# SwiGLU's hidden columns in five chunks of 512 and one mixed chunk of 256 gate and 256 up columns, in place of four of 512 and two of 384

## The chip, the cores and the metric

The kernel runs on one core of one Trainium2 chip. The metric is the device time of one execution in microseconds (us). An execution is also recorded by the hardware profiler; its page and its trace give the start and the duration of every instruction on the core's engines: TensorE (PE for matmuls, PEld for weight loads), VectorE (DVE), ScalarE (ACT), GpSimd (POOL), and SyncE (SP), which here issues loads.

## What is computed

A two-layer encoder trunk over 256 tokens of 1024 features, in float32. Each layer adds half a SwiGLU, a mixer, and half a SwiGLU to `x`; a final norm follows. Cut to what matters here:

```python
def swiglu(h, w_gate, w_up, w_down):      # 1024 x 2816, 1024 x 2816, 2816 x 1024
    return (jax.nn.silu(h @ w_gate) * (h @ w_up)) @ w_down

for layer in range(2):
    x = x + 0.5 * swiglu(rms_norm(x, ffn1_norm[layer]), ...)
    x = x + mixer(rms_norm(x, mix_norm[layer]))      # attention, even and odd layer differ
    x = x + 0.5 * swiglu(rms_norm(x, ffn2_norm[layer]), ...)
out = rms_norm(x, final_norm)
```

So there are six stages, numbered 0 to 5; the four SwiGLU stages are 0, 2, 3 and 5.

## The kernel before

**Precision by three products.** A float32 matrix product is made of three passes. Each weight is split into a high part (`hi`, a rounded copy that ACT makes, `high_part`, L461) and a low part (`lo`, the difference, by DVE, `low_part`, L464). Activations are split the same way (`th`, `tl` for the normalised input, `g_h`, `g_l` for the hidden values). `mm` (L444) then issues three matmuls into one accumulator, L453 to L455; this is a *triple*. The stationary operand is a 128 x 128 block of activations, the moving operand up to 512 columns of weights.

**The columns of a SwiGLU stage.** `ffn` (L629) goes through `FF_CHUNKS` (L31), the widths into which the 2816 hidden columns are cut. For a plain chunk it takes the 8 row blocks of the gate weights (`self.take(KD)`), runs `project` (L572) for both token tiles (128 tokens each), 8 triples each, and does the same for the up weights. `silu` (L640) runs on ACT one triple after a gate product is complete, `glu` (L644) on DVE one triple after the up product; 14 triples later (`GLU_WAIT`) the result is transposed on TensorE (`transposed`, L651) and split into `gT`, the operands of the down product. Some of the 512-wide chunks (`SEVEN`, L80: chunk 2 in stages 0 and 5, chunks 1 and 3 in stages 2 and 3) go through `seven_gates` (L729), which uses a Strassen scheme with seven products for gate and up together, and prepares sums of the input for it in `x_sums` (L699). These sums are kept in places that are needed only later: the split hidden values of later chunks (`g0_...`), and where there are fewer than four of them, a place of later pair sums (`k...`).

**The down product.** After the chunks the stage takes pairs of row blocks of `w_down` in the order of `DOWN` (L34), some as plain products, some by the Strassen scheme (`seven`, L873). The four accumulators `Y` stand in the banks `o`, `pj`, `s` and `s`.

**Banks.** `BANKS` (L121): two of `pj`, three of `s`, one `o`, two `tp`, each of 512 float32 columns; banks of one name are used in turn. A plain chunk takes `s`, `s` for the gates and `pj`, `pj` for the ups (after a Strassen chunk `pj`, `s`, `s`, `pj`).

**Supply of weights.** `plan` (L288) lists the loads in order of use. A unit is one raw tile of up to a megabyte; there are three (`RAWS`). A unit's load is issued on SP's queue by `load` (L356) when the first split of an earlier unit is begun. `supply` (L402) splits two row blocks at a time into `hi` and, a triple later, `lo`; up to seven such splits may be alive (`FIT`). How often that happens is paced by the triples: each adds `self.rate` to `self.due` in `tick` (L267), and when two blocks are due and there is room, a split is made. A split that is needed sooner is made at once. All engines run their instructions in the order in which the program issues them.

Of the kernel before, what the change touches and what calls it, by code (L numbers as in the profile page):

```python
# [17 lines left out]
P = 128  # L18
T = 256
NT = 2  # L20
D = 1024
KD = D // P
# [5 lines left out]
THETA = 10000.0  # L28
NEG = -1e30
SCALE = HD ** -0.5  # L30
FF_CHUNKS = [512, 512, 512, 512, 384, 384]  # L31


DOWN = {  # L34
# [154 lines left out]
def pairs(stage):  # L189
    return [({"p": "plain", "s": "strassen"}[o[0]], int(o[1:])) for o in DOWN[stage].split()]  # L190
# [9 lines left out]
class Trunk:  # L200
# [87 lines left out]
    def plan(self):  # L288


        a = self.a

        def columns(w2d, spans, units=None, kind="narrow"):
            w = sum(n for _, n in spans)
            k = 0
            for nk in units or (4, 4):
                pieces, o = [], 0
                for c0, n in spans:
                    src = w2d[k * P : (k + nk) * P, c0 : c0 + n].rearrange("(k p) n -> p k n", p=P)
                    pieces.append(((slice(0, P), slice(0, nk), slice(o, o + n)), src))  # L300
                    o += n
                yield pieces, nk, w, [2], kind
                k += nk

        def ffn(n, l, stage):
            c0 = 0
            for ci, w in enumerate(FF_CHUNKS):
                first = stage == 0 and c0 == 0
                if ci in SEVEN[stage]:
                    for k in range(0, KD, 2):  # L310
                        pieces = []
                        for i, name in enumerate(("_w_gate", "_w_up")):
                            src = a[n + name][l][k * P : (k + 2) * P, c0 : c0 + w].rearrange("(k p) n -> p k n", p=P)
                            pieces.append(((slice(0, P), slice(0, 2), slice(i * w, i * w + w)), src))
                        yield pieces, 2, D, [2], "strassen" if k >= KD - 2 * SEVEN[stage][ci] else "wide"
                    c0 += w
                    continue
                yield from columns(a[n + "_w_gate"][l], [(c0, w)], FIRST if first else None, "narrow" if first else "wide")
                yield from columns(a[n + "_w_up"][l], [(c0, w)], None, "wide")
                c0 += w  # L320
            for i, (kind, pair) in enumerate(pairs(stage)):
                src = a[n + "_w_down"][l][2 * pair * P : 2 * (pair + 1) * P, :].rearrange("(k p) n -> p k n", p=P)
                uses = [2, 3 if stage == 5 and i >= len(pairs(stage)) - HELD else 2]
                yield [(slice(0, P), src)], 2, D, uses, "wide" if kind == "plain" else kind

        def even():
            w_in, w_out = a["even_w_in"][0], a["even_w_out"][0]
            for spans in ([(512, 256), (1280, 256)], [(768, 512)], [(0, 512)]):
                yield from columns(w_in, spans)
            for g in (1, 0):  # L330
                for nh in range(2):
                    pieces = []
                    for s in range(2):
                        r0 = g * 512 + s * 256
                        src = w_out[r0 : r0 + 256, nh * 512 : nh * 512 + 512].rearrange("(j p) n -> p j n", p=HD)
                        pieces.append((slice(64 * s, 64 * s + 64), src))
                    yield pieces, 4, 512, [2], "narrow"

        def odd():
            w_qkv, w_out = a["odd_w_qkv"][0], a["odd_w_out"][0]  # L340
            for g in range(2):
                for i in (1, 0, 2):
                    yield from columns(w_qkv, [(i * D + g * 512, 512)])
            for g in range(2):
                for nh in range(2):
                    src = w_out[g * 512 : g * 512 + 512, nh * 512 : nh * 512 + 512].rearrange("(j p) n -> p j n", p=P)
                    yield [(slice(0, P), src)], 4, 512, [2], "narrow"

        yield from ffn("ffn1", 0, 0)
        yield from even()  # L350
        yield from ffn("ffn2", 0, 2)
        yield from ffn("ffn1", 1, 3)
        yield from odd()
        yield from ffn("ffn2", 1, 5)
# [233 lines left out]

    def first_gates(self, W):

# [29 lines left out]
        for j in range(KD // 2):  # L620
# [3 lines left out]
            for k in (2 * j, 2 * j + 1):  # L624
                for tt in range(NT):
                    self.mm(ps[tt], now.hT[tt][k], W[k], k == 0, k == KD - 1)
        return ps

    def ffn(self):  # L629
# [5 lines left out]
        tasks = []  # L635

        paired = {2 * pair: [] for kind, pair in down if kind == "strassen"}
        sums = {}

        def silu(tt, w, g, s):  # L640
            yield 1
            nc.scalar.activation(s[:, :w], g[:, :w], AF.Silu, scale=self.rstd_of(tt))

        def glu(tt, f0, w, u, s):  # L644
            yield 1
            m = self.t([P, 512], "glu", 2)
            nc.vector.scalar_tensor_tensor(m[:, :w], u[:, :w], self.now.r[tt], s[:, :w], op0=ALU.mult, op1=ALU.mult)
            yield GLU_WAIT
            yield from transposed(tt, f0, w, m)
# [49 lines left out]
        def x_sums():  # L699

            yield SEVEN_WAIT[self.now.n]
            gap = SEVEN_GAP[self.now.n]
            X = []
            for tt in range(NT):
                while len(self.now.hT[tt]) < KD:
                    yield 1
                x = self.t([P, 2, 512], ("shi", "slo")[tt], FIT["sum"], F32R).bitcast(F32)
                X.append(x.rearrange("p a (k t) -> p (a k) t", t=P)[:, : 2 * most, :])
                hi, lo = (t.bitcast(F32)[:, KD - 2 * most :, :] for t in self.hts[self.now.n, tt])
                nc.vector.tensor_tensor(X[tt], hi, lo, op=ALU.add)  # L710
                yield gap
            k0, k1, k2, k3 = (X[tt][:, i::2, :] for tt in range(NT) for i in range(2))
            for o, x, y, op in [
                (k2, k3, k2, ALU.subtract), (k3, k3, k1, ALU.subtract), (k1, k2, k1, ALU.subtract), (k0, k1, k0, ALU.add)
            ]:
                nc.vector.tensor_tensor(o, x, y, op=op)
                yield gap

            places = [(f"g0_{sum(FF_CHUNKS[:ci]) // P}_", FF_CHUNKS[ci] // P) for ci in range(max(sevens), len(FF_CHUNKS))]
            if len(places) < 4:  # L720
                places.append((f"k{max(paired)}", 4))
            for (tag, n), k in zip(places, (k0, k1, k2, k3)):
                hi, lo = (self.t([P, n, P], tag + p, 1, F32R)[:, :most, :] for p in "hl")
                self.high_part(hi, k)
                yield gap
                self.low_part(lo, k, hi)
                K.append([(hi[:, q, :], lo[:, q, :]) for q in range(most)])
# [98 lines left out]

        f0 = 0
        self.spawn(x_sums())
        for ci, w in enumerate(FF_CHUNKS):
            if ci in sevens:  # L830
                seven_gates(f0, w, sevens[ci])
                f0 += w // P
                continue
            self.rate = (AHEAD_RATE if ci + 1 in sevens else RATE)[self.now.n]

            tags = ["pj", "s", "s", "pj"] if ci - 1 in sevens else ["s", "s", "pj", "pj"]
            G = self.take(KD)
            S = []
            if self.now.n + ci == 0:
                both = self.first_gates(G)  # L840
            for tt in range(NT):
                g = both[tt] if self.now.n + ci == 0 else self.project(self.ready(tt), G, tags[tt])
                S.append(self.t([P, 512], "silu", 2))
                self.start(silu(tt, w, g, S[tt]))
            U = self.take(KD)
            for tt in range(NT):
                u = self.project(self.now.hT[tt], U, tags[NT + tt])
                tasks.append(self.start(glu(tt, f0, w, u, S[tt])))
            f0 += w // P
        W = {}  # L850

        parts = [[slice(0, 512), slice(512, 1024)] for _ in range(NT)]
# [7 lines left out]
        def use(f, tt, sl, last=False, to=None):  # L860
# [4 lines left out]
            if to is not None:  # L865
                self.mm(to, gT[tt][f], W[f][i], f == held[0], last, at)
                return
            self.mm(Y[tt][i][:, at], gT[tt][f], W[f][i], (tt, i) not in begun, last, at)
            begun.add((tt, i))
# [56 lines left out]
        for i, (kind, pair) in enumerate(down[:-HELD]):  # L926
# [6 lines left out]
            for f in (2 * pair, 2 * pair + 1):  # L933
                W[f] = self.take(2)
                for tt in range(NT):
# [6 lines left out]
        for f in held:  # L942
            W[f] = self.take(2)
        for tt in range(NT):
# [588 lines left out]
```

## Time and profile before

| | us |
|---|---|
| device time, median of 3 runs (956.24 to 956.81) | 956.25 |
| span of the profiled execution, first to last instruction | 954.4 |
| TensorE busy | 942.5 |
| VectorE busy | 791.9 |
| ScalarE busy | 585.3 |

The span of the profiled execution is 1.85 us shorter than the median of the runs, since it counts from the first to the last instruction. The page calls an engine busy while one of its instructions is under way. Matmuls overlap in it: each lasts longer than the distance to the next one's start, so that what a matmul costs in a row of matmuls is read from start to start. In a view of groups a row names the line, the engine, the operation, what it writes and reads and its shape, the count, the busy time in us and the mean of one in ns, and then the idle time of the engine ahead of it with what ended it. In a timeline a row is start, duration (of a merged row: of all its instructions), engine and line. The view by windows gives for each stretch its length, then for each engine the busy time and the number of instructions, then the granted clock, the busy share of the DMA engines and what they moved.

### The profile page before, as it was taken

Reading aid. Unit: us, or ns where it says so; the run is one execution under the profiler, and the core shown is the slowest. Engines: PE = TensorE matmul, PEld = TensorE weight load, DVE = VectorE, ACT = ScalarE, POOL = GpSimd, SP = SyncE. Lnnn points to the kernel's source line nnn. Section 1 sums busy time; section 2 is a strip of 40 time slices with the busy share of each in tenths; the row PEclk is TensorE's granted clock in tenths of the full one; section 3 lists DMA queues with packets and bytes.
Section 4 is the critical chain, followed back from the end, with each engine's and each line's share of the span. In section 5 each row is a group of like instructions: output and inputs, shape, how many; then the busy total and the mean of one; then the engine's idle time right before and its main releaser. Section 6 shows DMA issues by size and latency. Waiting matters only on the chain.

```text
span 954.4 us, 13005 instructions
## 1 busy us (share of the span) xinstructions
PE 942.5 (99%) x4767; PEld 795.7 (83%) x4767; DVE 791.9 (83%) x1244; ACT 585.3 (61%) x1011; POOL 95.3 (10%) x152
## 2 busy tenths in 40 slices
PE   9999999999999999999999999999999999999997
PEld 6888998877778889988888899888878888889886
DVE  6989777788869998787988888889877697996797
ACT  7555555477777565655646456557877585556453
POOL 1130000073420000000100000006130000000001
PEclk9999999999999999999999999999999999999999
DMA  8846665644425654766456476564624365466461
GB/s 289 267 135 204 204 214 176 218 132 94 128 89 176 216 193 143 243 220 217 145 168 199 151 217 222 198 242 137 202 97 145 121 201 196 134 207 201 165 242 44
DMA packets 82752, 171.65 MB, mean 180 GB/s; under 512 B 4096, under 2 KB 25344, under 8 KB 82688
## 3 DMA queue, kind: packets, MB, share of 16 engines
q1 hardware_dynamic: 82112, 170.04, 53.7%
q8 instruction: 37, 0.61, 0.3%
q10 hardware_dynamic: 576, 0.79, 0.2%
q14 instruction: 27, 0.22, 0.1%
HBM read 169.76 MB, written 1.05 MB: 179 GB/s over the span
## 4 chain that ended last, share of the span: by engine, by line
PE 90%; DVE 4%; ACT 3%; issue 1%; DMA 1%; POOL 1%; SPq 0%; POOLq 0%; DVEq 0%; ACTq 0%
PE pj L453 13%; PE pj L455 12%; PE pj L454 12%; PE s L454 11%; PE s L455 11%; PE s L453 11%; PE tp L531 3%; PE o L454 2%; PE o L455 2%; PE o L453 2%; PE o L1006 2%; DVE lo L464 2%; PE tp L1085 1%; PE tp L453 1%; PE tp L454 1%; PE tp L455 1%
## 5 line engine op out<-in xcount | busy, mean ns | idle before, releaser
L464 DVE TENSOR_TENSOR lo<-raw,hi 128x1024 fp32r<-128x1024 f32 (+2 forms) x388 | 375.9, 991 | 66.0 <-ACT hi L461 64.0
L461 ACT ACTIVATE hi<-raw 128x1024 fp32r<-128x1024 f32 (+2 forms) x388 | 320.5, 862 | 81.2 <-PE s L455 22.2
L453 PE MATMUL pj<-hi,th 128*128 128x512 f32 (+1 forms) x431 | 164.6, 382 | 0.0
L454 PE MATMUL pj<-lo,th 128*128 128x512 f32 (+1 forms) x431 | 161.1, 374 | 0.1
L455 PE MATMUL pj<-hi,tl 128*128 128x512 f32 (+1 forms) x431 | 161.1, 374 | 0.0
L453 PE MATMUL s<-hi,th 128*128 128x512 f32 (+1 forms) x373 | 142.0, 381 | 0.2 <-ACT hi L461 0.2
L454 PE MATMUL s<-lo,th 128*128 128x512 f32 (+1 forms) x373 | 139.0, 373 | 0.3 <-DVE lo L464 0.2
L455 PE MATMUL s<-hi,tl 128*128 128x512 f32 (+1 forms) x373 | 138.8, 372 | 0.0
L455 PEld LDWEIGHTS pj<-hi,tl 128*128 128x128 f32 x431 | 80.9, 188 | 12.2
L453 PEld LDWEIGHTS pj<-hi,th 128*128 128x128 f32 x431 | 81.0, 188 | 11.4 <-issue 0.9
L454 PEld LDWEIGHTS pj<-lo,th 128*128 128x128 f32 x431 | 81.1, 188 | 10.9 <-DVE lo L464 0.5
L454 PEld LDWEIGHTS s<-lo,th 128*128 128x128 f32 x373 | 70.2, 188 | 11.3 <-DVE lo L464 2.3
L455 PEld LDWEIGHTS s<-hi,tl 128*128 128x128 f32 x373 | 70.0, 188 | 9.8
L453 PEld LDWEIGHTS s<-hi,th 128*128 128x128 f32 x373 | 70.1, 188 | 9.3 <-ACT hi L461 0.4
L473 POOL TENSOR_TENSOR rstd<-var,mhalf 128x1 f32<-128x1 f32 (+2 forms) x16 | 17.1, 1069 | 592.7 <-DVE var L471 457.6
L461 ACT ACTIVATE shi<-two 128x1024 fp32r<-128x1024 f32 x30 | 31.8, 1059 | 41.6 <-DVE two L382 41.5
L464 DVE TENSOR_TENSOR slo<-raw,shi 128x1024 fp32r<-128x1024 f32 x30 | 36.6, 1221 | 20.5 <-ACT shi L461 20.5
L461 ACT ACTIVATE g_h<-tp 128x384 fp32r<-128x384 f32 (+1 forms) x48 | 25.7, 538 | 45.2 <-DVE quarters L679 24.4
L461 ACT ACTIVATE shi<-raw 128x1024 fp32r<-128x1024 f32 x30 | 31.7, 1058 | 33.2 <-PE s L455 19.1
L453 PE MATMUL s<-hi,g_h 128*128 128x512 f32 (+1 forms) x131 | 52.0, 397 | 0.0
L455 PE MATMUL s<-hi,g_l 128*128 128x512 f32 (+1 forms) x131 | 51.0, 389 | 0.0
L454 PE MATMUL s<-lo,g_h 128*128 128x512 f32 (+1 forms) x131 | 50.9, 388 | 0.0
(473 smaller groups left out, 1669.2 us busy)
## 6 DMA issues: line engine op xcount, KB each, us to landing
raw<-in_ffn_w_down SPq DMA_DIRECT2D x44, 1024.0 KB, 5.1
raw<-in_ffn_w_up SPq DMA_DIRECT2D x20, 1024.0 KB, 5.2
raw<-in_ffn_w_gate SPq DMA_DIRECT2D x18, 1024.0 KB, 5.1
raw<-in_ffn_w_gate SPq DMA_DIRECT2D x27, 512.0 KB, 3.9
raw<-in_ffn_w_up SPq DMA_DIRECT2D x24, 512.0 KB, 4.9
raw<-in_ffn_w_gate SPq DMA_DIRECT2D x16, 768.0 KB, 4.6
raw<-in_ffn_w_up SPq DMA_DIRECT2D x16, 768.0 KB, 4.8
raw<-in_odd_w_qkv SPq DMA_DIRECT2D x12, 1024.0 KB, 5.3
```

What stands on the lines that cost most here:

```text
L453: mm(ps, h, wh, start=first, stop=False)
L454: mm(ps, h, wl, start=False, stop=False)
L455: mm(ps, l, wh, start=False, stop=last)
L461: self.nc.scalar.activation(hi, src, AF.Copy)
L464: self.nc.vector.tensor_tensor(lo, src, hi.bitcast(F32), op=ALU.subtract)
L473: nc.gpsimd.tensor_tensor(r[:, :n], v[:, :n], self.mhalf[:, :n], op=ALU.pow)
L531: self.nc.tensor.transpose(tb[:, i * P : (i + 1) * P], src[:, i * P : (i + 1) * P], self.ident)
L1006: self.nc.tensor.matmul(O[64 * s : 64 * s + 64, i * P : i * P + P], v(b0 + i, s, kc), pT[s][:, i, kc, :], start=(kc == 0), stop=(kc == 1),)
L1085: nc.tensor.transpose(tb[:, o : o + P], p[:, i, kc * P : kc * P + P], self.ident)
```

## The change

The last two chunks of 384 columns become one of 512 and a rest of 256 (`FF_MIXED`). The rest is loaded so that one tile of 512 columns holds 256 of the gate and 256 of the up weights: two units of four row blocks, two loads each, taken after the last full chunk. One product of 8 triples per token tile fills one bank `s` with both; `silu` reads its first half and `glu` its second half. The places of `x_sums` follow the new list of chunks, and where it is too short any number of places of later pair sums is appended, the last first.

```diff
-FF_CHUNKS = [512, 512, 512, 512, 384, 384]
+FF_CHUNKS = [512, 512, 512, 512, 512]
+FF_MIXED = 256
...
                 yield from columns(a[n + "_w_gate"][l], [(c0, w)], FIRST if first else None, "narrow" if first else "wide")
                 yield from columns(a[n + "_w_up"][l], [(c0, w)], None, "wide")
                 c0 += w
+            for k in range(0, KD, 4):
+                pieces = []
+                for i, name in enumerate(("_w_gate", "_w_up")):
+                    src = a[n + name][l][k * P : (k + 4) * P, c0 : c0 + FF_MIXED].rearrange("(k p) n -> p k n", p=P)
+                    pieces.append(((slice(0, P), slice(0, 4), slice(i * FF_MIXED, (i + 1) * FF_MIXED)), src))
+                yield pieces, 4, 2 * FF_MIXED, [2], "wide"
...
             places = [(f"g0_{sum(FF_CHUNKS[:ci]) // P}_", FF_CHUNKS[ci] // P) for ci in range(max(sevens), len(FF_CHUNKS))]
-            if len(places) < 4:
-                places.append((f"k{max(paired)}", 4))
+            places += [(f"k{f}", 4) for f in sorted(paired, reverse=True)]
...
                 tasks.append(self.start(glu(tt, f0, w, u, S[tt])))
             f0 += w // P
+
+        w, V = FF_MIXED, self.take(KD)
+        for tt in range(NT):
+            both = self.project(self.now.hT[tt], V, "s")
+            s = self.t([P, 512], "silu", 2)
+            self.start(silu(tt, w, both, s))
+            tasks.append(self.start(glu(tt, f0, w, both[:, w:], s)))
         W = {}
```

## The prediction

> **What bounds the kernel now.** First the page: its head, the share of each engine, the granted clock, and the engines of the chain that ended last.
>
> ```profile
> span 954.4 us, 13005 instructions
> ...
> PE 942.5 (99%) x4767; PEld 795.7 (83%) x4767; DVE 791.9 (83%) x1244; ACT 585.3 (61%) x1011; POOL 95.3 (10%) x152
> ...
> PEclk9999999999999999999999999999999999999999
> ...
> PE 90%; DVE 4%; ACT 3%; issue 1%; DMA 1%; POOL 1%; SPq 0%; POOLq 0%; DVEq 0%; ACTq 0%
> ```
>
> TensorE is busy in 99% of the span at full clock and makes up 90% of the chain. So the change can help only if it makes TensorE's own work shorter or takes away one of its few waits; work that it saves on DVE or ACT counts only where TensorE waits for them. But matmuls overlap, so "busy" also hides short waits. I therefore look at the stretches that the change rewrites, the two chunks of 384 columns in each of the four SwiGLU stages (0, 2, 3, 5), in the view by windows:
>
> ```profile
> core 0: us, PE busy (x) PEld busy (x) DVE busy (x) ACT busy (x) POOL busy (x), PEclk, DMA share, GB/s
> 97.50:132.30 34.80, 34.80 (x207) 34.64 (x206) 23.32 (x31) 20.18 (x29) 0.00 (x0) 1.00 0.62 212
> 370.00:404.80 34.80, 34.80 (x207) 34.65 (x206) 27.78 (x41) 21.14 (x34) 0.00 (x0) 1.00 0.71 237
> 552.75:588.05 35.30, 35.26 (x207) 34.51 (x206) 29.26 (x42) 21.78 (x34) 0.00 (x0) 1.00 0.77 257
> 855.15:889.95 34.80, 34.80 (x207) 34.62 (x207) 24.83 (x35) 20.68 (x31) 0.00 (x0) 1.00 0.62 212
> ```
>
> The first number is the length of the stretch. Three stages take 34.80 us for it and stage 3 takes 35.30, so there TensorE loses 0.5 us to waits; elsewhere it runs through. DVE is busy 67 to 83% of the time: nothing here is limited by it. What one matmul really costs is the distance between starts, which the timeline of TensorE shows (stage 0, the change from 512 to 384 columns):
>
> ```profile
> 94.80 0.39 PE L453 MATMUL pj<-hi,th 128*128 128x512 f32 x1
> ...
> 97.52 0.33 PE L453 MATMUL s<-hi,th 128*128 128x384 f32 x1
> ...
> 98.59 0.33 PE L453 MATMUL s<-hi,th 128*128 128x384 f32 x1
> ...
> 101.19 0.60 PE L531 MATMUL tp<-mats,glu 128*128 128x128 f32 x4
> ```
>
> From 94.80 to 97.52 stand 12 matmuls of 512 columns, from 98.59 to 101.19 stand 15 of 384. So one of 512 takes 2.72 / 12 = 226.7 ns and one of 384 takes 2.60 / 15 = 173.3 ns. The 128 columns between them cost 53.3 ns, 0.417 ns each. By that 512 columns are 213.3 ns and 384 are 160 ns: **about 13.3 ns of each matmul do not depend on its columns.** This is the term that the change acts on.
>
> **The change part by part.** *Matmuls.* Before, the two chunks take per stage 2 chunks x 2 (gate, up) x 2 token tiles x 8 row blocks x 3 products = 192 matmuls of 384. After, a chunk of 512 takes 96 and the mixed one, with gate and up side by side in one bank, 8 x 2 x 3 = 48, all of 512: 144. The columns are the same (192 x 384 = 144 x 512 = 73,728). Times: 192 x 173.3 = 33.28 us, 144 x 226.7 = 32.64 us. Saved: 0.64 us per stage, **2.56 us in four stages**, wholly on the path since TensorE does not wait here. The counts agree with the six groups of 384 in the view by line, each x128 (768 in all, 4 x 192); the first and the last stand below, with the rows of the other engines that the change resizes.
>
> The Trainium skill, "TensorE: Matmul & The Clock Gate", section "Wait — 56ns, not 53.3ns?", speaks against this size: it gives a fixed cost of about 2.5 ns for a warm matmul. By it the 192 matmuls fewer would bring 192 x 2.5 = 0.48 us, an estimate from that page, and nothing to measure. The rows above differ from it (13.3 ns, with a weight load before each matmul); it is kept as a rival.
>
> ```profile
> L453 PE MATMUL s<-hi,th 128*128 128x384 f32 x128 | 44.2, 345 | 0.0
> ...
> L455 PE MATMUL pj<-hi,tl 128*128 128x384 f32 x128 | 42.8, 334 | 0.0
> ...
> L464 DVE TENSOR_TENSOR lo<-raw,hi 128x1024 fp32r<-128x1024 f32 x182 | 218.1, 1220 | 32.4 <-ACT hi L461 31.8
> L461 ACT ACTIVATE hi<-raw 128x1024 fp32r<-128x1024 f32 x182 | 186.6, 1053 | 53.1 <-PE pj L455 17.2 <-PE s L455 14.5 <-DMA raw<-in_ffn_w_up 7.4
> ...
> L464 DVE TENSOR_TENSOR lo<-raw,hi 128x768 fp32r<-128x768 f32 x64 | 59.2, 952 | 15.2 <-ACT hi L461 14.6
> L461 ACT ACTIVATE hi<-raw 128x768 fp32r<-128x768 f32 x64 | 51.2, 838 | 10.0 <-DMA raw<-in_ffn_w_up 5.3 <-PE s L455 2.8 <-PE pj L455 1.8
> ...
> L647 DVE SCALAR_TENSOR_TENSOR glu<-pj,rstd,silu 128x512 f32<-128x512 f32 x16 | 11.9, 743 | 0.1
> L642 ACT ACTIVATE silu<-s,rstd 128x512 f32<-128x512 f32 x16 | 10.9, 684 | 1.0 <-PE s L455 0.5
> ...
> L647 DVE SCALAR_TENSOR_TENSOR glu<-pj,rstd,silu 128x384 f32<-128x384 f32 x14 | 8.5, 611 | 1.4 <-PE pj L455 1.4
> L642 ACT ACTIVATE silu<-s,rstd 128x384 f32<-128x384 f32 x14 | 8.1, 578 | 0.0
> ```
>
> *High and low parts.* Per stage 16 splits of 768 elements become 12 of 1024: DVE 16 x 952 = 15.2 to 12 x 1220 = 14.6 us, ACT 13.4 to 12.6 us. On the path this is worth nothing where TensorE does not wait. Per matmul triple the supply stays as it was, because the rate counts triples (a pair of row blocks serves four): a low part of 1.22 us in 4 x 0.68 us instead of one of 0.95 us in 4 x 0.52 us. Everything else that DVE and ACT do in these ticks (the sums after a Strassen chunk, 512 columns each) keeps its size and gets 0.16 us more per tick.
>
> *Stage 3's wait.* There the supply is tight:
>
> ```profile
> 559.16 0.85 ACT L461 ACTIVATE hi<-raw 128x768 fp32r<-128x768 f32 x1 [2.72 <-DMA raw<-in_ffn_w_up]
> ...
> 562.37 0.72 ACT L782 ACTIVATE glu<-glu,rstd 128x512 f32<-128x512 f32 x1 [2.37 <-DVE glu L780]
> ...
> 564.56 2.69 DVE L464 TENSOR_TENSOR lo<-raw,hi 128x768 fp32r<-128x768 f32 x3
> ...
> 565.11 0.42 PE L453 MATMUL s<-hi,th 128*128 128x384 f32 x1
> 565.54 0.37 SPq L366 DMA_DIRECT2D raw<-in_ffn_w_up  x1
> 565.57 0.44 PE L454 MATMUL s<-lo,th 128*128 128x384 f32 x1
> ```
>
> ACT waits first for a weight load, then behind the sums, the low part comes at about 565.5, and the matmul at 565.57 starts 0.46 us after its predecessor, where 0.17 is usual. After the change TensorE gets to this product, the 23rd triple of its chunk, 22 x 0.16 = 3.5 us later. The load awaited at 559.16 and the one before it carry 0.52 MB more, 2.0 us at this stretch's 257 GB/s (an estimate), and the four splits behind it take DVE 4 x 0.27 = 1.1 us longer. The 0.4 us that remain about cover the wait. I take 0.4 of stage 3's 0.5 us; the bounds are 0.5 gained and, if the loads come slower still, 0.4 lost.
>
> *The mixed chunk's own wait.* Before, `silu` of a gate ran 16 triples ahead of its `glu`. Now both come one triple after the same product, so DVE stands at `glu` until ACT has done `silu`. By the step from 512 to 384 columns, 256 cost 684 - 2 x 106 = 472 ns on ACT and 743 - 2 x 132 = 479 ns on DVE (estimates). So DVE is held some 0.5 us longer, twice a stage. Queued behind it on DVE are the low parts of the first down pairs, and TensorE would wait for those. How long they are ready ahead, in stage 3, where it is least:
>
> ```profile
> 580.10 2.36 DVE L464 TENSOR_TENSOR lo<-raw,hi 128x1024 fp32r<-128x1024 f32 x2 [1.05 <-ACT hi L461]
> ```
> ```profile
> 588.43 0.40 PE L454 MATMUL o<-lo,g_h 128*128 128x512 f32 x1
> ```
>
> Half of the 2.36 us is the first low part, done at 581.3 and read at 588.43: 7.1 us of cover for a hold of about 1 us. Cost: nothing; without the cover 4 x 1 us. The `glu` work itself is the same (4 x 611 = 2444; 2 x 743 + 2 x 479 = 2444 ns). The banks do not bind: the mixed chunk takes two of the three banks `s`, and the first down product into one of them (`Y[1][1]`) comes 11 triples, 7.5 us, after the product that `glu` must have read.
>
> *Loads and places.* The stage keeps eight load instructions for these columns on SP's queue: 8 of 768 KB become 4 of 1024 and 4 of 512 KB, in rows of 1 KB for the mixed chunk. Rows of that shape:
>
> ```profile
> raw<-in_ffn_w_up SPq DMA_DIRECT2D x20, 1024.0 KB, 5.2
> ...
> raw<-in_ffn_w_up SPq DMA_DIRECT2D x16, 768.0 KB, 4.8
> ...
> raw<-in_even_w_in SPq DMA_DIRECT2D x4, 512.0 KB, 6.0
> ```
>
> The last are 1 KB rows, two issues to a unit, and land in 6.0 us. A mixed unit lands between 6 and 12 us (both at once, or one after the other); I take 6 to 7, as its megabyte is no more than the 1024 KB of the 5.2 us row. Splits are made up to seven ahead, so it is hidden. `x_sums` now puts one or two of its four operands into the places of later pair sums (`k14`, `k16`, `k12`): the same instructions, and those sums are written only 14 triples after the Strassen chunk that read the operands. Nothing.
>
> **Sum.** Against the profiled execution: 954.4 - 2.56 - 0.4 = 951.4 us of span. The runs' median of 956.25 is 1.85 us above that span; with it, **953.3 us**, 0.3% faster. A difference below 0.2% (1.9 us) cannot be told from none here, so the border is at 954.3.
>
> **Rivals.**
> *A, the forecast*: fixed part of each matmul goes, stage 3's wait goes. 952.7 to 954.3, chance 0.71.
> *B, part of it is eaten by supply*: stages 2 and 3, with DVE at 80 and 83% and loads at 0.71 and 0.77 of the DMA engines, keep or double their wait: the saving of these two (1.3 us) and stage 3's 0.4 are lost, 953.3 + 1.7 = 955.0. For it: the two waits of ACT above. Against: TensorE comes later to each split. 0.17.
> *C, nothing per matmul is saved*: the 13.3 ns belong to the columns after all (a bank filled to its end, say), so that only stage 3's wait goes: 956.25 - 0.4 = 955.85. Against: the two pitches above, measured side by side. 0.06. By the 2.5 ns of the Trainium skill's page the time would be 956.25 - 0.48 = 955.8, an estimate from it.
> *D, slower*: the mixed chunk's loads, rows of 1 KB, are late. Place: its second unit, for which TensorE's fourth row pair waits. Point: the 7.1 us of cover; if the two issues of a unit land one after the other, at 12 us, and the unit before delays them by as much, 6 + 6 - 7.1 = 4.9 us are lost in the worst stages 2 and 3, 2 x 4.9 in all: 953.3 + 9.8 = 963. Against: the view of waits names no load among what matmuls waited for. 0.06.
>
> **How the numbers follow.** Predicted is A, 953.3. Faster by over 0.2%: A, 0.71. Within 0.2%: B and C, 0.23. Slower: D, 0.06. The range takes in A and B, 0.88, cut to 952.5 to 955.2: below by the 0.1 us that is left of stage 3's wait, 0.2 us for 1 ns of reading error in the fixed cost (192 x 1 ns) and the 0.5 us or so by which runs of one kernel lie apart (956.24 to 956.81), above by B's time.
>
> **What would show it.** Right: 4575 matmuls in place of 4767; the stretch of these columns 0.6 us shorter in stages 0, 2, 5 and about 1 us in stage 3; 226.7 ns between matmuls of the mixed chunk; no TensorE wait at the start of the down products. Wrong: a pitch above 227 ns in the mixed chunk (C or bank trouble), waits of TensorE for `lo` in stages 2 and 3 (B), waits of ACT `hi` for `in_ffn_w_gate` or `in_ffn_w_up` that reach TensorE in the mixed chunk (D), or a time over 954.3 with the stretches as forecast, which would put the loss elsewhere.

## The result, and the profile after

| | before | after |
|---|---|---|
| median of 21 runs, us | 956.24 (955.35 to 956.86) | 954.83 (954.05 to 955.55) |
| ratio, 95% interval | | 0.9984 [0.9978, 0.9991] |
| profiled execution: span, us | 954.4 | 952.3 |
| TensorE matmuls | 4767 | 4575 |

The kernel is 1.4 us faster (ratio 0.9984, so 0.16%): less than half of the forecast's 3.0 us, inside its range (952.5 to 955.2), and on the other side of the 0.2% border. The profiled execution of after is itself one of the quicker ones (954.08 us), so the spans differ by 2.1 us where the medians differ by 1.4. The page's head and engine shares after:

```profile
span 952.3 us, 12568 instructions
...
PE 939.0 (99%) x4575; PEld 770.2 (81%) x4575; DVE 790.9 (83%) x1228; ACT 583.2 (61%) x995; POOL 94.4 (10%) x152
```

TensorE's busy time fell by 3.5 us, the span by 2.1: some of what was saved came back as waiting. To find where, I cut both traces into the six stages, each from TensorE's first transposition of `x` to the next stage's (stage 0 from the first product, the last one to the start of the last matmul). Worked out from the traces, in us:

| stage | before | after | difference | forecast |
|---|---|---|---|---|
| 0 SwiGLU | 179.85 | 178.84 | -1.01 | -0.64 |
| 1 mixer | 91.29 | 91.32 | +0.03 | 0 |
| 2 SwiGLU | 181.20 | 180.58 | -0.62 | -0.64 |
| 3 SwiGLU | 182.57 | 181.59 | -0.98 | -1.04 |
| 4 mixer | 120.36 | 120.40 | +0.04 | 0 |
| 5 SwiGLU | 185.52 | 186.30 | +0.78 | -0.64 |

The six differences add up to -1.76 us; another 0.39 us of the spans' difference lies ahead of the first product (7.10 and 6.71 us into the span), where the change does nothing.

Stages 2 and 3 did what was forecast to within 0.06 us. Stage 5 did not: it is 1.42 us longer than forecast. The view by windows shows that its chunks are not the cause. The four rows are the last 512 chunk and the mixed one in stages 0, 2, 3 and 5 (columns as before):

```profile
96.73:131.27 34.54, 34.54 (x161) 28.60 (x160) 23.52 (x27) 20.04 (x25) 0.00 (x0) 1.00 0.55 188
368.64:403.20 34.56, 34.56 (x161) 28.60 (x160) 28.25 (x35) 20.85 (x28) 0.00 (x0) 1.00 0.66 225
550.71:585.44 34.73, 34.73 (x162) 28.60 (x160) 29.19 (x37) 19.94 (x28) 0.00 (x0) 1.00 0.76 247
852.27:886.84 34.57, 34.57 (x162) 28.60 (x161) 24.10 (x28) 19.11 (x26) 0.00 (x0) 1.00 0.56 186
```

Stage 5's stretch is as short as those of stages 0 and 2, and TensorE is busy in all of it; stage 3's has 0.2 us of waits, where 0.5 were before. (From the first matmul of the stretch to the first of the down product stage 0 took 34.92 us before. The 34.54 us now hold two transposes of 0.11 us more, which the down product has less, so the stretch saves 0.60 us; by the same reckoning stages 2 and 5 save 0.6 and stage 3 saves 0.9.) The loss is behind it, in the down product. TensorE's waits after name it, in the view of waits (what waited, line, for what; total, times, longest):

```profile
PE o L1468 <- DVE zeros L1462: 1.5, 1, 1.5
PE tp L460 <- DVE g_l L471: 1.1, 1, 1.1
```

The second row is new. It is one matmul, and the timeline of all engines shows which:

```profile
899.84 1.22 DVE L471 TENSOR_TENSOR lo<-raw,hi 128x1024 fp32r<-128x1024 f32 x1
...
900.05 0.39 PE L462 MATMUL pj<-hi,k4l 128*128 128x512 f32 x1
...
900.98 0.42 DVE L471 TENSOR_TENSOR g_l<-tp,g_h 128x256 fp32r<-128x256 f32 x1
...
901.31 1.22 DVE L471 TENSOR_TENSOR slo<-two,shi 128x1024 fp32r<-128x1024 f32 x1
...
901.54 0.47 PE L460 MATMUL tp<-shi,k4h 128*128 128x512 f32 x1 [1.10 <-DVE g_l L471]
```

From 900.05 to 901.54 TensorE starts nothing: 1.49 us where 0.23 is usual, 1.27 us lost. The matmul that waits is the fourth product of the first Strassen pair, and the first that goes into a bank `tp` (`temp("7", "tp", ...)`, in `seven`). Both banks `tp` hold the transposed results of the mixed chunk, one for each token tile, until DVE has read them for their low parts (`g_l`). Before, the same two instructions stood 2.4 us apart (the low part ends at 901.42, the product starts at 903.82):

```profile
900.87 0.55 DVE L464 TENSOR_TENSOR g_l<-tp,g_h 128x384 fp32r<-128x384 f32 x1
...
903.82 0.39 PE L453 MATMUL tp<-shi,k4h 128*128 128x512 f32 x1
```

On the clock of the span the low part came at the same time in both. TensorE came 3.5 us sooner: the stage began 2.9 us earlier and the chunks took 0.6 us less. DVE did not move up with it. Why, its own timeline shows, from the start of the down product (after: 886.84) on:

```profile
889.05 0.42 DVE L686 TENSOR_TENSOR quarters<-tp,quarters 128x256 f32<-128x256 f32 x1
890.50 0.48 DVE L654 SCALAR_TENSOR_TENSOR glu<-s,rstd,silu 128x256 f32<-128x256 f32 x1 [1.03 <-ACT silu L649]
891.45 1.23 DVE L471 TENSOR_TENSOR slo<-two,shi 128x1024 fp32r<-128x1024 f32 x1 [0.46 <-ACT shi L468]
892.59 0.69 DVE L471 TENSOR_TENSOR g_l<-tp,g_h 128x512 fp32r<-128x512 f32 x1
893.19 0.28 DVE L693 TENSOR_TENSOR quarters<-quarters 128x128 f32<-128x128 f32 x1
893.51 0.29 DVE L694 TENSOR_TENSOR quarters<-quarters 128x128 f32<-128x128 f32 x1
894.56 0.69 DVE L471 TENSOR_TENSOR k16l<-quarters,k16h 128x512 fp32r<-128x512 f32 x1 [0.76 <-ACT k16h L468]
895.51 1.23 DVE L471 TENSOR_TENSOR slo<-raw,shi 128x1024 fp32r<-128x1024 f32 x1 [0.26 <-ACT shi L468]
```

`quarters` and `k16` are the sums for the down product's pair 8, whose columns lie in the last 512 chunk. Here DVE makes them in the first 8.4 us of the down product. Before, the same work was over when the down product began (890.11):

```profile
885.99 0.29 DVE L687 TENSOR_TENSOR quarters<-quarters 128x128 f32<-128x128 f32 x1
887.04 0.69 DVE L464 TENSOR_TENSOR k16l<-quarters,k16h 128x512 fp32r<-128x512 f32 x1 [0.76 <-ACT k16h L461]
```

A chunk of 384 still followed, 32 triples with gates and ups; now only the mixed chunk does, 16 triples. The sums come as many triples after their product as ever, so they have moved from inside the chunks to the head of the down product, where DVE also has the sums of the Strassen weights to make. They do not only add work there. The sums go to and fro between DVE and ACT (`quarters`, `k16h`, `k16l`), and DVE stands still while ACT does its part: from the start of the down product to the end of the awaited low part DVE takes 14.56 us, where it took 11.31 before, and 2.51 us of it are the four waits for ACT in the rows above, of which before has none. So much is read; that it is the cause had to be shown.

### The profile page after: what moved, and what is told of

Read it like the earlier page. It is cut to its first block, busy times and chain, and to the rows that moved or that the text cites. A ratio compares the mean times of both kernels' runs of the same rounds, so it can differ in the third digit from the quotient of the medians.

```text
span 952.3 us, 12568 instructions
## 1 busy us (share of the span) xinstructions
PE 939.0 (99%) x4575; PEld 770.2 (81%) x4575; DVE 790.9 (83%) x1228; ACT 583.2 (61%) x995; POOL 94.4 (10%) x152
## 4 chain that ended last, share of the span: by engine, by line
PE 89%; DVE 5%; ACT 3%; issue 1%; DMA 1%; POOL 0%; POOLq 0%; ACTq 0%; DVEq 0%
PE s L461 12%; PE s L462 12%; PE s L460 12%; PE pj L460 12%; PE pj L462 11%; PE pj L461 11%; PE tp L538 2%; PE o L460 2%; PE o L462 2%; PE o L461 2%; DVE lo L471 2%; PE o L1019 2%; PE tp L1098 1%; PE tp L460 1%; PE tp L462 1%
## 5 line engine op out<-in xcount | busy, mean ns | idle before, releaser
L471 DVE TENSOR_TENSOR lo<-raw,hi 128x1024 fp32r<-128x1024 f32 (+1 forms) x372 | 374.2, 1027 | 64.2 <-ACT hi L468 61.4
L468 ACT ACTIVATE hi<-raw 128x1024 fp32r<-128x1024 f32 (+1 forms) x372 | 317.9, 890 | 76.4 <-PE s L462 26.3
L460 PE MATMUL s<-hi,th 128*128 128x512 f32 x373 | 149.1, 400 | 0.4 <-ACT hi L468 0.4
L460 PE MATMUL pj<-hi,th 128*128 128x512 f32 x367 | 146.7, 400 | 0.0
L461 PE MATMUL s<-lo,th 128*128 128x512 f32 x373 | 145.8, 391 | 0.3 <-DVE lo L471 0.2
L462 PE MATMUL s<-hi,tl 128*128 128x512 f32 x373 | 145.9, 391 | 0.0
L461 PE MATMUL pj<-lo,th 128*128 128x512 f32 x367 | 143.2, 390 | 0.1
L462 PE MATMUL pj<-hi,tl 128*128 128x512 f32 x367 | 143.3, 390 | 0.0
L462 PEld LDWEIGHTS pj<-hi,tl 128*128 128x128 f32 x367 | 68.9, 188 | 14.7
L468 ACT ACTIVATE g_h<-tp 128x512 fp32r<-128x512 f32 (+2 forms) x48 | 25.7, 537 | 42.4 <-DVE quarters L686 28.1
```

What stands on the lines that cost most here:

```text
L460: mm(ps, h, wh, start=first, stop=False)
L461: mm(ps, h, wl, start=False, stop=False)
L462: mm(ps, l, wh, start=False, stop=last)
L468: self.nc.scalar.activation(hi, src, AF.Copy)
L471: self.nc.vector.tensor_tensor(lo, src, hi.bitcast(F32), op=ALU.subtract)
```

## The experiments

Theory **T1**: TensorE waits for bank `tp` since DVE reaches the mixed chunk's `g_l` too late, behind the pair sums of the last 512 chunk. **T2**: it is the hold of 1.03 us alone, DVE standing at `glu` for `silu`. **T3**: the place waits for something else, a load or split of its pair. **T4**: not the sums stand ahead of `g_l`, but the weight splits that the stage's rate of 0.68 makes early. All edits below are on the changed kernel; differences are of medians against the kernel before as timed with each group (the changed kernel: -1.41), and of stage 5's length against before (the changed kernel: +0.78).

| kernel | median | of before | ratio, 95% interval | difference | stage 5 |
|---|---|---|---|---|---|
| e1_glu_later | 955.09 | 955.98 | 0.9990 [0.9981, 0.9998] | -0.89 | +1.18 |
| e2_turn_early | 953.30 | 955.98 | 0.9972 [0.9961, 0.9984] | -2.68 | -0.71 |
| e3_stage5_old | 953.50 | 955.98 | 0.9975 [0.9964, 0.9985] | -2.48 | -0.01 |
| e4_order5 | 954.49 | 955.98 | 0.9986 [0.9977, 0.9995] | -1.49 | +0.63 |
| e5_plain8 | 953.77 | 955.87 | 0.9978 [0.9970, 0.9987] | -2.10 | +0.07 |
| e6_turn10 | 953.96 | 955.87 | 0.9979 [0.9970, 0.9988] | -1.91 | +0.43 |
| e7_quarters | 957.07 | 955.87 | 1.0015 [1.0006, 1.0024] | +1.20 | +1.57 |
| e8_turn_late_stages | 952.85 | 955.87 | 0.9968 [0.9956, 0.9981] | -3.02 | -0.68 |

The intervals are 1.6 to 2.4 us wide, as much as most of the versions lie apart. So what an edit did is read above all from the waits and from the length of stage 5, of one profiled execution each; the medians point the same way.

**Without the hold (e1).** `glu` of the mixed chunk comes later, its transposes at the same triple.

```diff
-        def glu(tt, f0, w, u, s):
-            yield 1
+        def glu(tt, f0, w, u, s, ahead=1, wait=GLU_WAIT):
+            yield ahead
...
-            yield GLU_WAIT
+            yield wait
...
-            tasks.append(self.start(glu(tt, f0, w, both[:, w:], s)))
+            tasks.append(self.start(glu(tt, f0, w, both[:, w:], s, 4, GLU_WAIT - 3)))
```

> The mixed chunk's glu comes four triples after its product instead of one, and its transposes at the same triple as before, so that silu is long done and DVE no longer stands 1.03 us for ACT. Theory T1 (stage 5's 1.27 us wait of TensorE comes from the whole queue that DVE has ahead of the first token tile's g_l, above all the pair sums of the last 512 chunk, which have lost the second half of a chunk to hide in): the wait shrinks by less than the hold and most of it stays, 0.4 to 1.2 us. Rival T2 (it is the hold at glu alone): the wait is gone or under 0.3 us, time 1 us below the changed kernel.

The wait did not shrink, it grew. The view of waits, and then DVE's timeline:

```profile
PE tp L460 <- DVE g_l L471: 1.5, 1, 1.5
```
```profile
892.49 1.23 DVE L471 TENSOR_TENSOR slo<-two,shi 128x1024 fp32r<-128x1024 f32 x1 [1.98 <-ACT shi L468]
```

DVE now stands 1.98 us at the next instruction that needs ACT, where it had stood 1.03 and 0.46. ACT comes late to both because it has itself waited for DVE's `quarters` just before, as its timeline in e1 shows:

```profile
890.54 0.60 ACT L468 ACTIVATE g_h<-tp 128x512 fp32r<-128x512 f32 x1 [3.28 <-DVE quarters L686]
```

An idle gap taken out in one place opened in the next. T2 falls as it stands: the hold at `glu` is gone and the wait is not. What e1 does not take out is DVE's standing for ACT as such: 1.98 + 0.76 us here, 2.51 us in the changed kernel. (This profiled execution has 0.7 us more in stage 4 too, where ACT waited longer for `rs`, 5.3 us in place of 4.3, and TensorE then 0.5 us for ACT; the edit does not touch that stage.)

**Transposes earlier (e2).** With the same `wait` argument as in e1, and only this in the call:

```diff
-            tasks.append(self.start(glu(tt, f0, w, both[:, w:], s)))
+            tasks.append(self.start(glu(tt, f0, w, both[:, w:], s, 1, 6)))
```

> The mixed chunk is transposed 6 triples after its glu instead of 14, so its high and low parts stand 8 triples (5.4 us) earlier in the queues of ACT and DVE. T1 and T2 both: the bank tp is free in time, stage 5's wait of 1.27 us is gone, time about 1 us below the changed kernel (0.9975 of the kernel before). Rival T3 (the wait at that place is for something else, the load of the pair or its split): it stays.

The wait for `tp` is gone and stage 5 lands on its forecast, -0.71. T3 falls. It costs something in stage 0, where the transposes now come before DVE is done with `glu` (waits of TensorE, e2):

```profile
PE tp L538 <- DVE glu L654: 0.9, 2, 0.6
```

Of these 0.9 us the kernel before and the changed one have 0.3, in stage 2.

**Stage 5 cut as before (e3).** The lists of chunks become lists for each stage; the core of the edit:

```diff
+CHUNKS = {n: [512, 512, 512, 512, 512] for n in (0, 2, 3)}
+CHUNKS[5] = [512, 512, 512, 512, 384, 384]
+MIXED = {0: 256, 2: 256, 3: 256, 5: 0}
```

> Stages 0, 2 and 3 as changed, stage 5 cut as in the kernel before. T1, T2: the 1.27 us wait is gone and stage 5's 0.64 us saving too, so 0.6 us below the changed kernel. If stage 5 costs nothing in truth (the profile showed one execution's accident): 0.6 us above the changed kernel.

Stage 5 is back at its old length (-0.01), the kernel 1.07 us below the changed one by the differences (-2.48 against -1.41), more than the 0.6 expected. Its seven runs (953.29 to 954.00) lie below all 21 of the changed kernel (954.05 to 955.55), which were timed with a before only 0.26 us slower. So in stage 5 the change costs more than it brings, and it is no accident of one profiled execution.

**First Strassen pair later (e4).**

```diff
-    5: "p3 p0 s2 s5 p4 s1 p9 s7 s8 p6 p10",
+    5: "p3 p0 p4 s2 s5 s1 p9 s7 s8 p6 p10",
```

> In stage 5 one plain pair more goes ahead of the first Strassen pair, which so comes 24 instead of 16 triples after the mixed chunk; nothing else is changed. T1, T2: its first product in bank tp comes 5.5 us later and finds the bank free, the 1.27 us wait is gone. T3: the wait moves along with the Strassen pair. Later waits may come from the changed order of splits.

The wait for `tp` went, and T3 falls again. The time hardly moved (stage 5 +0.63): near the end of the stage two products now wait for `lo`, 0.4 and 0.3 us from start to start, and with the late starts beside them about 1.1 us is lost there, most of the 1.27. It may be because the last Strassen pairs have one plain pair less among them (not tried). As a repair it fails.

**Pair 8 plain (e5).**

```diff
-    5: "p3 p0 s2 s5 p4 s1 p9 s7 s8 p6 p10",
+    5: "p3 p0 s2 s5 p4 s1 p9 s7 p8 p6 p10",
```

> In stage 5 pair 8, whose columns lie in the last 512 chunk, is multiplied plainly instead of by the Strassen scheme: eight triples instead of seven (0.68 us more on TensorE), and no pair sums of that chunk on DVE and ACT at the start of the down product. T1 (these sums stand ahead of the mixed chunk's g_l): the wait for bank tp in stage 5 is gone, so stage 5 is 1.27 us shorter and 0.68 us longer, 0.6 us below the changed kernel. Rival T4 (the splits that the rate of 0.68 puts into DVE's queue early are the cause, not the sums): the wait stays at about 1 us and the stage is 0.5 us longer.

No wait for `tp`; stage 5 is 0.71 us below the changed kernel's, as expected of T1 (0.6), with rate, splits ahead of the place and the mixed chunk as they were. DVE's timeline in e5:

```profile
889.67 0.47 DVE L654 SCALAR_TENSOR_TENSOR glu<-s,rstd,silu 128x256 f32<-128x256 f32 x1
...
896.66 0.42 DVE L471 TENSOR_TENSOR g_l<-tp,g_h 128x256 fp32r<-128x256 f32 x1
```

The low part starts 4.32 us earlier than in the changed kernel. With the sums all four waits for ACT are gone, the hold at `glu` among them: 2.51 us, more than the sums' own work on DVE. This shows the pair sums, with the waits that they bring, as what stands in the way, and T4 falls: the early splits alone do not make TensorE wait. How much of the loss the sums' work would cost without the waits, no run separates.

**Transposes ten triples after `glu` (e6).** As e2, with 10 in place of 6.

> The mixed chunk's transposes come 10 triples after its glu, in place of 14, in all four stages. T1: g_l of the first token tile comes some 2.7 us earlier in DVE's queue, more than the 1.27 us missing in stage 5, whose wait is gone; stage 0 gets no wait of the transposes for glu (0.73 us with 6 triples). 1.3 us below the changed kernel.

Half right: 0.50 us below the changed kernel by the medians, for 1.3 expected. The fourth product found its bank, but the seventh (`temp("6", "tp", ...)`), which takes the other bank `tp`, waited for the second token tile's low part (waits of TensorE, e6):

```profile
PE tp L460 <- DVE g_l L471: 0.7, 1, 0.7
```

DVE's timeline in e6:

```profile
897.15 0.42 DVE L471 TENSOR_TENSOR g_l<-tp,g_h 128x256 fp32r<-128x256 f32 x1
...
902.94 0.42 DVE L471 TENSOR_TENSOR g_l<-tp,g_h 128x256 fp32r<-128x256 f32 x1
```

The first low part starts 3.83 us sooner than in the changed kernel (900.98), the second one 0.50 us later (902.44 there). So both banks are late, and ten triples help one of them alone.

**The fixed part of a matmul by itself (e7).** The same 256 columns in two mixed chunks of 128 + 128, 96 matmuls of 256 in place of 48 of 512:

```diff
-FF_MIXED = 256
+FF_MIXED = 128
...
-        w, V = FF_MIXED, self.take(KD)
-        for tt in range(NT):
+        w = FF_MIXED
+        for half in range(2):
+          V = self.take(KD)
+          for tt in range(NT):
...
+          f0 += 1
```

> The last 256 columns go in two mixed chunks of 128 gate and 128 up columns: 96 matmuls of 256 per stage instead of 48 of 512. If each matmul costs 13.3 ns beside its columns: 120 ns from start to start, the 96 take 11.52 us instead of 10.88, 0.64 us more per stage. If nothing is fixed: 113 ns, no more time. If the weight load of 188 ns bounds it: 188 ns and 7.2 us more per stage.

Its timeline of TensorE in stage 2, twelve matmuls apart:

```profile
396.65 0.28 PE L463 MATMUL s<-hi,tl 128*128 128x256 f32 x1
...
398.09 0.28 PE L463 MATMUL s<-hi,tl 128*128 128x256 f32 x1
```

1.44 / 12 = 120.0 ns, the value that 13.3 ns and 0.417 ns a column give. Against the changed kernel the stages grew by 0.68 (stage 0), 0.58 (stage 2), 0.38 (stage 3) and 0.79 us (stage 5), for 0.64 expected; why stage 3 grew by less is not known.

**Only where the Strassen pair comes early (e8).** As e2, with `6 if self.now.n in (3, 5) else GLU_WAIT` as the wait: stages 3 and 5 start their first Strassen pair 16 triples into the down product, stage 0 after 24, stage 2 after 32.

> The mixed chunk's transposes come 6 triples after its glu in stages 3 and 5 (first Strassen pair after 16 triples) and 14 in stages 0 and 2. T1: no wait for bank tp in stage 5, none of transposes for glu in stage 0; stages 0.6 to 0.7 us below the kernel before in 2 and 5, about 1.2 in 3. 1.4 us below the changed kernel, 953.4.

No wait of stage 5, and none of the transposes for `glu` in stage 0, is left in what TensorE waited for; these are the longest, all of them also in the kernel before:

```profile
PE o L1468 <- DVE zeros L1462: 1.4, 1, 1.4
PE tp L1098 <- ACT pt L994: 0.8, 1, 0.8
PE tp L1098 <- DVE okTx L471: 0.7, 1, 0.7
```

Stages 0, 2, 3 and 5 are at -1.03, -0.65, -0.93 and -0.68 us (for stage 3 about -1.2 was expected). At 952.85 us (0.9968, five runs) its median is the lowest here, 3.0 us below the kernel before: the gain that the forecast gave to the change itself. By its interval it cannot be told from e2.

## Why the prediction was right or wrong

**What bounds the kernel: right.** In stages 2 and 3 a change to TensorE's own work showed in the time to within 0.1 us; a saving on DVE and ACT (1.0 and 2.1 us less busy) showed nowhere.

**13.3 ns per matmul, 0.64 us a stage: right in size.** Stage 2, where nothing else happens, gives 0.62, and the pitch in the mixed chunk after is again 2.72 us for 12 matmuls:

```profile
127.18 0.39 PE L462 MATMUL s<-hi,tl 128*128 128x512 f32 x1
...
129.90 0.39 PE L462 MATMUL s<-hi,tl 128*128 128x512 f32 x1
```

With e7 rival C (nothing fixed) is out, and so is the 2.5 ns of the Trainium skill ("TensorE: Matmul & The Clock Gate", "Wait — 56ns, not 53.3ns?") for this stream of float32r matmuls, each with its own weight load. Three widths lie on one line: 120.0, 173.3 and 226.7 ns.

**Stage 3's wait: right.** 0.34 us of it went (0.98 less 0.64); I took 0.4 of 0.5.

**The mixed chunk's own wait: wrong, and this is the step that failed.** The hold was mis-sized, 1.03 us against 0.5, because `silu` queues on ACT behind a `g_h` that itself waits for DVE; what that alone would have cost no run shows, since in e1 the gap only moved. What I missed is what was behind the hold. I named the low parts of the down pairs, with 7.1 us of cover, and I wrote "The banks do not bind", having looked at the banks `s` alone. The banks `tp` did bind: `g_l` is queued on DVE like the low parts, and the first Strassen pair needs its bank. And the prediction has nothing on the pair sums of the last 512 chunk; of DVE's and ACT's other work it says only that it keeps its size. Halving what follows that chunk moved them, with 2.51 us of waits for ACT, to the head of the down product. The two rows of before that would have told me are above: `g_l` at 900.87 and the product at 903.82, a cover of 2.4 us in stage 5, not 7.1. The prediction's last sign of being wrong, a time over 954.3 with the stretches as forecast, is what came.

**Rivals.** What happened is B in kind, a saving eaten by DVE's queue, but in stage 5 and over a bank, not in stages 2 and 3 over `lo`; it cost 1.4 us where B had 1.7. D did not happen: no wait of TensorE for a load in the rewritten part. The range held by luck, because B's price was in it, not because the loss that came was foreseen; the likeliest case (0.71) did not come. Rival C's second figure, 955.8, leaves out stage 3's 0.4 us, which its first figure takes off; with it that figure is 955.4.

**Open.** Stage 0 is 0.37 us shorter than forecast in the changed kernel, and 0.2 to 0.4 in e1, e3, e5, e6 and e8. 0.2 of it is a wait for `lo` around 70 us that is shorter after; for the rest there is a single profiled execution of before to compare with. And stage 3, with the same pair 8 and the same 16 triples, has no wait: its cover fell from 2.9 to 1.6 us (low part 10.83 and 11.90 us into the down product, bank needed at 13.69 and 13.47). Why stage 5 lost about 2 us more is only read from its order on DVE, where a Strassen split (`slo` at 891.45) comes ahead of the last sums: DVE stands for ACT 2.51 us there, and in stage 3 only at `glu`, 1.03 us, as its timeline shows. No run tried it.

## What to carry to other kernels

When a chunk is made smaller or dropped, list what was timed by counting steps *after* the chunk before it: that work keeps its distance and lands in the next phase, beside work that it never met. For each accumulator bank that the next phase takes, find the last reader of its old content and measure its cover in the trace, queue by queue; one bank that is free early says nothing of another. And fewer, wider matmuls are worth the fixed part of each, which two widths side by side in a timeline give to a tenth of a microsecond per stage.

## What the runs showed of the hardware

In e7 matmuls start 120 ns apart while each one's weight load is shown as 0.19 us long; in its timeline of weight loads they start 120 ns apart as well:

```profile
396.65 0.19 PEld L461 LDWEIGHTS s<-hi,th 128*128 128x128 f32 x1
396.77 0.19 PEld L462 LDWEIGHTS s<-lo,th 128*128 128x128 f32 x1
396.89 0.19 PEld L463 LDWEIGHTS s<-hi,tl 128*128 128x128 f32 x1
```

So a load row of 188 ns does not bound the pitch: the rows of loads overlap one another, and their durations added up come to more than the time in which they ran. What was expected of e7 had left that bound open (7.2 us more a stage).
